# Gate and up products of a decoder layer taken by pairs of column chunks, three of eight k-tile pairs as 2 by 2 block products with seven multiplications

## The chip, the core and the metric

The kernel runs on one core of one Trainium2 chip. The metric is the device time of one execution in microseconds (us). The engines of the core are TensorE (PE in the profile, with its weight loads as PEld), VectorE (DVE), ScalarE (ACT), GpSimd (POOL) and SyncE (SP), whose queue issues most DMAs. SBUF is the memory that the engines read, PSUM the one that PE writes its products to, in eight banks of 128 partitions x 512 float32.

## The reference

One layer of a decoder for 256 tokens of width 2048, in float32. `w_gate` and `w_up` are 2048 x 5632, `w_down` is 5632 x 2048, and there are two feed-forwards:

```python
def swiglu(x, w_gate, w_up, w_down):
    return (jax.nn.silu(x @ w_gate) * (x @ w_up)) @ w_down

x = layer_norm(A * x + 0.5 * swiglu(x, ffn1 ...), ln1 ...)   # A = 2 ** 0.25
# token mixing: one input projection (2048 x 3416), 8 heads of latent attention,
# 8 heads of sparse attention with three gated branches, one output projection (2048 x 2048)
x = layer_norm(A * x + mix, ln2 ...)
x = layer_norm(A * x + 0.5 * swiglu(x, ffn2 ...), ln3 ...)
```

## The kernel before

**Three passes.** Each float32 operand is split into a high part of 12 bits and the rest. `split` (lines 74 to 76) does it with a cast on ACT (L75) and a subtraction on DVE (L76). A product of one k-tile, one token tile and one chunk of 512 columns is then `mm3` (lines 78 to 82): three matmuls, high by high (L80), high by low (L81), low by high (L82).

**Tiles.** The 256 tokens are two tiles of 128 (`t` = 0, 1). The 2048 inputs are 16 k-tiles of 128, loaded as eight pairs. The 5632 hidden columns are 11 chunks of 512. `load` (lines 120 to 138) brings a pair of k-tiles of one chunk, 512 KB, into a `raw` buffer (pool `rawp`, five) with a DMA on SP's queue, and splits it into `whi` and `wlo` (pools `hip` and `lop`, six buffers each of 128 x 1024).

**One product.** `gemm` (lines 143 to 183) takes one chunk of columns for both token tiles, each with a PSUM bank of the pool `acc` (four). Pair by pair it loads the weights and issues 2 k-tiles x 2 token tiles x 3 matmuls, then `finish` takes the banks. After each pair it calls `tick(2)`. The logical clock of ticks decides after which pieces the small side tasks (generators started by `spawn`) put their next instructions on PE; their banks come from the pool `msc` (four).

**Feed-forward.** `ffn` (lines 243 to 286) goes through the chunks in groups of 4, 4 and 3. For each chunk it does the gate product (`gate`: silu of the bank on ACT, L253), the up product (`up`: multiplied by the gate's result on DVE, L258), and `DFF` = 4 ticks later four transposes of that result for each token tile (L262), whose bank is split again into a `thi`/`tlo` pair. After a group, the down product accumulates the group's chunks, with `y` updated on DVE (L280, L282). `begin` and `after` load x, the constants and the residual in the first feed-forward; `late` calls `ln_res` (lines 342 to 350), which applies the gain and bias of the layer norm before to `y`, once for each of the first four chunks.

**Layer norm.** `ln` (lines 324 to 340) normalises `y` and transposes it by `norm_T` (lines 302 to 317) into the `x1` or `x2` pairs that the next products read. The first product after it takes eight pieces for token tile 0 before token tile 1 (`head`).

**What sets the order.** PE and SP run their instructions in the order of the program text. For DVE, ACT and POOL a planner orders the instructions when the kernel is built, by the order of the text and by its own estimate of when each is ready; the buffer of a pool that a tile gets is chosen in the same pass. Each engine then works its list in order. The order within a bank or a buffer is kept by semaphores.

Of the kernel before, what the change touches and what calls it, by code (L numbers as in the profile page):

```python
# [11 lines left out]
F32 = mybir.dt.float32  # L12
# [6 lines left out]
P = 128  # L19
D = 2048  # L20
S = 256
NT = S // P
# [14 lines left out]
NM = 12  # L37
DFF, DTR, DEV, DLN, DSM = 4, 7, 2, 4, 4
# [3 lines left out]
def layer(ctx: ExitStack, tc: tile.TileContext, a: dict, out: bass.AP):  # L42
# [4 lines left out]
    rawp = ctx.enter_context(tc.tile_pool(name="rawp", bufs=5))  # L47
# [11 lines left out]
    W = {n: (a[n], (k // P) // KT, w) for n, (k, w) in _CHUNKS.items()}  # L59

# [24 lines left out]
    lanes, now, flags = {}, [0], {}  # L85
# [34 lines left out]
    def load(w, c, pc, spare=False):  # L120
        """k-tiles pc of column chunk c of w, each as (hi, lo); `spare` takes them from the mixer's tiles"""
        ap, pairs, n = w
# [4 lines left out]
        nc.sync.dma_start(raw[:, :kn, :n], ap[r0:r0 + P].rearrange("p (k n) -> p k n", k=KT)[:, k0 % KT:k0 % KT + kn])  # L127
        if spare:
            out = []
            for j in range(kn):  # L130
                hi, lo = (am(F32R).rearrange("p a b -> p (a b)")[:, :n] for _ in range(2))
                split(hi, lo, raw[:, j, :n])
                out.append((hi, lo))
            return out
# [3 lines left out]
        return [(hi[:, j, :n], lo[:, j, :n]) for j in range(kn)]  # L138

    def new_acc():  # L140
        return acc.tile([P, NCH], F32, name="acc")

    def gemm(x, w, c, ks, finish, head=0, tail=0, spare=0, first=KT, each=None):
        """finish(t, ps): ps [128 tokens of tile t, n] = sum over k in ks of x[k, t].T @ w[k, column chunk c]

        The two token tiles alternate by piece of w, but for the first `head` and the last `tail` pieces,
        where tile 0 takes them all before tile 1.
        """
        n = w[2]
        ps = [new_acc()[:, :n] for _ in range(NT)]  # L150
# [33 lines left out]

    def new_T():
        return (tp.tile([P, 4, P], F32R, name="thi"), tp.tile([P, 4, P], F32R, name="tlo"))
# [10 lines left out]

    def load_x(k, n=2):
        """n k-tiles of x"""
        raw = rawp.tile([P, KT, NCH], F32, name="raw")  # L200
        nc.sync.dma_start(raw[:, :n, :S], a["xT"][k * P:(k + n) * P, :].rearrange("(k p) n -> p k n", p=P))
        for t in range(NT):
            if k % 4 == 0:
                xT[k // 4, t] = new_T()
            hi, lo = xT[k // 4, t]
            j = k % 4
            split(hi[:, j:j + n, :], lo[:, j:j + n, :], raw[:, :n, t * P:(t + 1) * P])

    def load_consts():
# [15 lines left out]
        # key k of the second half against query p: k <= p  # L225
# [17 lines left out]
    def ffn(wg, wu, wd, x, done, begin=None, after=None, late=()):  # L243
        groups = [[0, 1, 2, 3], [4, 5, 6, 7], [8, 9, 10]]
        late = list(late)
        for gi, grp in enumerate(groups):
            hT = {}
            for c in grp:
                sg = {}

                def gate(t, ps):
                    sg[t] = work.tile([P, NCH], F32, name="sg")
                    A.activation(sg[t], ps, AF.Silu)  # L253

                def up(t, ps):
                    def go(c=c, sg=sg):
                        h = wk([P, NCH])
                        V.tensor_tensor(h, ps, sg[t], op=OP.mult)  # L258
                        yield DFF
                        pt = msc.tile([P, 4, P], F32, name="msc")  # L260
                        for j in range(4):
                            PE.transpose(pt[:, j, :], h[:, j * P:(j + 1) * P], ident)  # L262
                        hT[c, t] = new_T()
                        split(hT[c, t][0], hT[c, t][1], pt)

                    spawn(go())
                    steps()

                gemm(x, wg, c, list(range(KD)), gate, head=0 if c or begin else HEAD, spare=SPARE,
                     first=1 if c == 0 and begin else KT, each=begin if c == 0 else None)  # L270
                gemm(x, wu, c, list(range(KD)), up, each=after if c == 0 else None)
                if late:
                    late.pop(0)()
# [28 lines left out]
    def norm_T(src, gcol, bcol, dst, k0):  # L302
        """dst (hi, lo) [128 k, j, 128 tok] <- transpose of src [128 tok, j*128] scaled by columns"""
        pt = msc.tile([P, 4, P], F32, name="msc")
# [12 lines left out]
        split(dst[0][:, :nj, :], dst[1][:, :nj, :], v[:, :nj, :])  # L317

# [5 lines left out]
    def ln(t, name, eps, x):  # L324
        """x[n, t] <- layer norm of y, transposed; y <- y normalised, without gain and bias"""
# [11 lines left out]
        for n in range(4):  # L337
            x[n, t] = new_T()
            norm_T(yc[n], cst[name + "_g"], cst[name + "_b"], x[n, t], 4 * n)
            yield 1  # L340

    def ln_res(name, n):
        """y, normalised so far, to the layer norm's result"""
# [34 lines left out]
    def done1(t, n):  # L378
# [5 lines left out]
    ffn(W["ffn1_w_gate"], W["ffn1_w_up"], W["ffn1_w_down"], lambda k, t: sl(xT[k // 4, t], k % 4), done1,  # L384
        begin=begin, after=load_y)

# [5 lines left out]
    def rope(dst, ps, cos, sin, h, d):  # L392
        """dst [128, h, d] <- rotated ps [128, h, d]"""
# [35 lines left out]
    def fin_b(t, ps):  # L429
        def go():  # L430
# [12 lines left out]
            pt = msc.tile([P, 4, P], F32, name="msc")  # L443
# [14 lines left out]
    def fin_c(t, ps):  # L458
        def go():
# [5 lines left out]
            pt = msc.tile([P, 4, P], F32, name="msc")  # L465
# [38 lines left out]
    def causal(ps, t, nh, scale, gate):  # L504
        """ps [128 q, nh*K] scores -> pT [128 keys, kb, nh, 128 q]"""
# [8 lines left out]
        pt = msc.tile([P, NCH], F32, name="msc")  # L514
# [15 lines left out]
    def mla_proj(g):  # L530
# [3 lines left out]
        def fin_q(hp):  # L534
            def fin(t, ps):
                def go():
# [6 lines left out]
                    pt = msc.tile([P, 4, P], F32, name="msc")  # L543
# [11 lines left out]
        def fin_kv(hp):  # L555
            def fin(t, ps):
                def go():
# [5 lines left out]
                    pt = msc.tile([P, 4, P], F32, name="msc")  # L563
# [17 lines left out]
    def mla_att(g, qnT, qrT, knT, vm):  # L581
        def unit(t, h0, nh):
# [3 lines left out]
            ps = msc.tile([P, NCH], F32, name="msc")  # L586
# [7 lines left out]
            po = msc.tile([P, 4, P], F32, name="msc")  # L594
# [10 lines left out]
    # native sparse attention  # L605
# [7 lines left out]
    def fin_kv2(n):  # L613
        def fin(t, ps):
            def go():
# [5 lines left out]
                pt = msc.tile([P, 4, P], F32, name="msc")  # L621
# [11 lines left out]
    def q_proj(g):  # L633
        def fin(t, ps):
            def go():
# [3 lines left out]
                pt = msc.tile([P, 4, P], F32, name="msc")  # L639
# [11 lines left out]
    # compressed keys and values  # L651
# [3 lines left out]
    def compress(src, n):  # L655
# [10 lines left out]
        pa = new_acc()  # L666
# [13 lines left out]
        pt = msc.tile([P, 4, P], F32, name="msc")  # L680
# [14 lines left out]
        po = msc.tile([P, 4, P], F32, name="msc")  # L695
# [12 lines left out]
    def nsa_att(g):  # L708
        pcTs = {}

        def cmp(t):
            yield from until(("q", g, t), ("kcmp",))
            qT = qTs[g, t]
            ps = msc.tile([P, 4, P], F32, name="msc")
# [7 lines left out]
            pt = msc.tile([P, 4, P], F32, name="msc")  # L722
# [6 lines left out]
        # selected blocks (all of them, as their number is at most SEL_TOPK) and window (wider than SEQ)  # L729
        def unit(t, h0, nh):  # L730
# [3 lines left out]
            for bi, n in ((1, "sel"), (2, "win")):  # L734
                yield from until(*[(n, b) for b in range(t + 1)])
                ps = msc.tile([P, NCH], F32, name="msc")
# [4 lines left out]
                if bi == 1:  # L741
                    yield from until(("pc", g, t), ("vcmp",))
                    po = msc.tile([P, 4, P], F32, name="msc")
# [29 lines left out]
    x2 = {}  # L773

    def out_last(ks, ns):
        """these columns for tile 0, then for tile 1"""
        held = {}
        for t in range(NT):
            for n in ns:
                ps = new_acc()  # L780
# [8 lines left out]
            spawn(ln(t, "ln2", LN_EPS, x2))  # L789
# [23 lines left out]
    def done3(t, n):  # L813
# [11 lines left out]
    ffn(W["ffn2_w_gate"], W["ffn2_w_up"], W["ffn2_w_down"], lambda k, t: sl(x2[k // 4, t], k % 4), done3,  # L825
        late=[lambda n=n: ln_res("ln2", n) for n in range(4)])
# [13 lines left out]
# weights: rows, columns of a chunk  # L840
_CHUNKS = {"w_in": (D, NCH), "w_in_b": (D, 344), "mla_w_uq": (QR, 384), "mla_w_ukv": (KVR, NCH), "w_out": (D, NCH)}
for _n in ("ffn1", "ffn2"):
    _CHUNKS.update({f"{_n}_w_gate": (D, NCH), f"{_n}_w_up": (D, NCH), f"{_n}_w_down": (FF, NCH)})

# [40 lines left out]
```

## Time and profile before

| | us |
|---|---|
| median of three runs | 1838.82 (1837.93 to 1839.55) |
| span of the profiled execution | 1836.4 |
| PE busy | 1819.7 |
| DVE busy | 1019.5 |
| ACT busy | 815.7 |
| mean DMA rate | 191 GB/s |

The span runs from the first to the last instruction of one profiled execution; no other time of that execution is listed, and the median of the runs is 2.4 us above the span. The busy time of an engine is the time in which at least one of its instructions runs. Matmuls are pipelined and overlap in the records, so the mean duration of one is longer than the time that it adds to a row of them.

### The profile page before, as it was taken

The page shows a single profiled execution, that of the slowest core. Times are in us where ns is not written, and L with a number is a line of the kernel's source. Part 1 is how long each engine was busy: PE and PEld are TensorE (multiplying, and loading weights), DVE is VectorE, ACT ScalarE, POOL GpSimd, SP SyncE. Part 2 cuts the span into 40 slices and gives each one's busy share as a digit, 9 for nine tenths or more (in the row PEclk, how much of TensorE's full clock was granted, in tenths as well). Part 3 has the DMA queues.
Part 4 walks back from the last instruction along what each step waited for, and adds up shares of the span by engine and source line. Part 5 has one row for each costly group of instructions (what it writes and reads, how often), then busy time and mean ns, then how long its engine had stood idle before and what let it go on. Part 6 is the DMA issues. An engine that isn't in the chain of part 4 may idle for free.

```text
span 1836.4 us, 21892 instructions
## 1 busy us (share of the span) xinstructions
PE 1819.7 (99%) x8394; PEld 1499.9 (82%) x8394; DVE 1019.5 (56%) x1253; ACT 815.7 (44%) x1071; POOL 17.7 (1%) x40
## 2 busy tenths in 40 slices
PE   8999999999999999999999999999999999999997
PEld 7888888888888888887788788888888888888886
DVE  5554554444554556766566687555455454545456
ACT  6444344444334444654555555444334444344431
POOL 0000000000000000000000000000000000000000
PEclk9999999999999999999999999999999999999999
DMA  9655565555555555566733347655665555555554
GB/s 341 226 194 174 193 204 194 186 184 183 195 195 185 193 186 182 170 186 217 267 104 127 126 161 231 201 187 185 194 195 194 185 194 186 194 193 189 191 192 138
DMA packets 102137, 349.98 MB, mean 191 GB/s; under 512 B 11136, under 2 KB 17296, under 8 KB 102032
## 3 DMA queue, kind: packets, MB, share of 16 engines
q1 hardware_dynamic: 100720, 344.37, 56.5%
q0 software_dynamic: 1312, 4.21, 1.0%
q8 instruction: 66, 1.08, 0.2%
q14 instruction: 39, 0.32, 0.1%
HBM read 346.44 MB, written 2.10 MB: 190 GB/s over the span
## 4 chain that ended last, share of the span: by engine, by line
PE 98%; DVE 1%; DMA 0%; ACT 0%; issue 0%; DVEq 0%; POOL 0%; ACTq 0%; POOLq 0%
PE acc L80 31%; PE acc L82 31%; PE acc L81 31%; PE msc L262 1%; PE msc L748 1%; PE msc L738 1%; PE msc L592 1%; PE acc L674 0%; PE msc L591 0%; PE msc L518 0%; PE msc L307 0%; PE msc L597 0%; DMA raw<-in_ffn_w_gate 0%; PE msc L745 0%; DVE wlo L76 0%
## 5 line engine op out<-in xcount | busy, mean ns | idle before, releaser
L76 DVE TENSOR_TENSOR wlo<-raw,whi 128x1024 fp32r<-128x1024 f32 (+3 forms) x604 | 733.3, 1215 | 721.5 <-ACT whi L75 720.3
L75 ACT CAST whi<-raw 128x1024 fp32r<-128x1024 f32 (+3 forms) x604 | 631.4, 1046 | 852.3 <-PE acc L82 805.7
L80 PE MATMUL acc<-whi,thi 128*128 128x512 f32 (+2 forms) x2414 | 945.2, 392 | 0.0
L81 PE MATMUL acc<-wlo,thi 128*128 128x512 f32 (+2 forms) x2414 | 936.3, 388 | 0.1
L82 PE MATMUL acc<-whi,tlo 128*128 128x512 f32 (+2 forms) x2414 | 936.4, 388 | 0.0
L80 PEld LDWEIGHTS acc<-whi,thi 128*128 128x128 f32 x2414 | 453.7, 188 | 95.7 <-issue 4.8
L82 PEld LDWEIGHTS acc<-whi,tlo 128*128 128x128 f32 x2414 | 453.4, 188 | 92.6
L81 PEld LDWEIGHTS acc<-wlo,thi 128*128 128x128 f32 x2414 | 453.8, 188 | 90.2 <-DVE wlo L76 0.8
L75 ACT CAST thi<-msc 128x512 fp32r<-128x512 f32 (+1 forms) x56 | 28.9, 556 | 37.4 <-PE msc L262 35.5
L80 PE MATMUL acc<-m,thi 128*128 128x512 f32 x98 | 39.2, 400 | 5.5 <-ACT m L75 4.7
L76 DVE TENSOR_TENSOR tlo<-msc,thi 128x512 fp32r<-128x512 f32 (+1 forms) x56 | 34.3, 645 | 17.6 <-ACT thi L75 17.6
L82 PE MATMUL acc<-m,tlo 128*128 128x512 f32 x98 | 38.9, 397 | 0.7 <-DVE tlo L76 0.7
L81 PE MATMUL acc<-m,thi 128*128 128x512 f32 x98 | 38.8, 396 | 0.0
L253 ACT ACTIVATE sg<-acc 128x512 f32<-128x512 f32 x44 | 26.3, 598 | 22.0 <-PE acc L82 21.9
L487 ACT ACTIVATE w<-w,mx 128x256 f32<-128x256 f32 (+1 forms) x48 | 21.4, 446 | 31.6 <-DVE mx L483 31.6
L76 DVE TENSOR_TENSOR m<-raw,m 128x512 fp32r<-128x512 f32 x49 | 31.6, 684 | 1.6 <-ACT m L75 1.6
L258 DVE TENSOR_TENSOR w<-acc,sg 128x512 f32<-128x512 f32 x44 | 28.3, 682 | 3.0 <-PE acc L82 3.0
L75 ACT CAST m<-raw 128x512 fp32r<-128x512 f32 x49 | 28.1, 617 | 2.7 <-DMA raw<-in_ffn_w_gate 2.7
L80 PEld LDWEIGHTS acc<-m,thi 128*128 128x128 f32 x98 | 18.7, 190 | 9.6 <-ACT m L75 4.7
L282 DVE TENSOR_TENSOR y<-acc,y 128x512 f32<-128x512 f32 x32 | 20.7, 682 | 9.9 <-PE acc L82 9.9
L82 PEld LDWEIGHTS acc<-m,tlo 128*128 128x128 f32 x98 | 18.7, 190 | 5.4 <-DVE tlo L76 1.6
L262 PEld LDWEIGHTS msc<-ident,w 128*128 128x128 f32 x176 | 20.5, 140 | 2.9
(144 smaller groups left out, 559.9 us busy)
## 6 DMA issues: line engine op xcount, KB each, us to landing
raw<-in_ffn_w_up SPq DMA_DIRECT2D x176, 512.0 KB, 3.3
raw<-in_ffn_w_down SPq DMA_DIRECT2D x176, 512.0 KB, 3.3
raw<-in_ffn_w_gate SPq DMA_DIRECT2D x175, 512.0 KB, 4.1
raw<-in_w_in SPq DMA_DIRECT2D x48, 512.0 KB, 4.4
raw<-in_w_out SPq DMA_DIRECT2D x32, 512.0 KB, 3.3
raw<-in_nsa_cmp_w_k SPq DMA_DIRECT2D x8, 512.0 KB, 4.1
raw<-in_nsa_cmp_w_v SPq DMA_DIRECT2D x8, 512.0 KB, 4.2
raw<-in_mla_w_uq SPq DMA_DIRECT2D x8, 384.0 KB, 3.9
```

The costliest lines, as they stand in the source:

```text
L75: A.copy(hi, src)
L76: V.tensor_tensor(lo, src, f(hi), op=OP.subtract)
L80: PE.matmul(ps, xh, wh, start=first, stop=False)
L81: PE.matmul(ps, xh, wl, start=False, stop=False)
L82: PE.matmul(ps, xl, wh, start=False, stop=last)
L253: A.activation(sg[t], ps, AF.Silu)
L258: V.tensor_tensor(h, ps, sg[t], op=OP.mult)
L262: PE.transpose(pt[:, j, :], h[:, j * P:(j + 1) * P], ident)
L282: V.tensor_tensor(y[t][:, cs], ps, y[t][:, cs], op=OP.add)
L487: A.activation(s[:, h, :], s[:, h, :], AF.Exp, bias=mx[:, h:h + 1], accum_out=sm[:, h:h + 1])
L592: PE.matmul(o, qrT[t][:, hh, :], krT[:, b, :], start=False, stop=True)
L738: PE.matmul(ps[:, h * K:(h + 1) * K], qT[:, h0 + h, :], kT[n][:, g, :K], start=True, stop=True)
```

## The change

**Algebra.** Chunks 0 to 9 of the gate and up weights are taken by pairs of chunks. For one pair of k-tiles (k, l), two token tiles and two chunks, the product is a 2 by 2 block product of eight `mm3`. In three of the eight pairs of k-tiles (`SEVEN` = 1, 3, 5) it is done with seven, in the way of Strassen and Winograd. With the weight blocks kn, lm, ln, km (k or l by chunk n or m) these are, by the bank that takes them:

- p1: x(k,0) kn; p5: s1 t1; p6: s2 t2; p7: s3 t3
- out(0,n): x(l,0) ln; out(0,m): s4 lm; out(1,n): x(l,1) t4; out(1,m): nothing
- t1 = kn + km, t3 = lm + km, t2 = t1 + lm, t4 = t2 + ln (three DVE instructions on raw weights, then split)
- s1 to s4: sums of the blocks of x, made once for each feed-forward in `sums`, split, and kept in six `m` tiles

After k-pair 5 DVE combines p1, p5, p6, p7 into four tiles (q = p6 + p1, u = p7 + q, v = p5 - q, z = p5 - u), and at the end of the product adds p1, v, u, z to the four output banks. The other five pairs take eight `mm3` into the four output banks.

**Where it is used.** `gemm2` does the gate products of the chunk pairs (2,3), (4,5), (6,7), (8,9) and the up products of those and of (0,1), in both feed-forwards. The gate products of chunks 0 and 1 stay with `gemm`, as do those of chunk 10 and all the others.

```diff
+NW = 11
+SEVEN = (1, 3, 5)
-    rawp = ctx.enter_context(tc.tile_pool(name="rawp", bufs=5))
+    rawp = ctx.enter_context(tc.tile_pool(name="rawp", bufs=6))
...
-    acc = ctx.enter_context(tc.tile_pool(name="acc", bufs=4, space=PSUM))
-    msc = ctx.enter_context(tc.tile_pool(name="msc", bufs=4, space=PSUM))
+    bank = ctx.enter_context(tc.tile_pool(name="bank", bufs=8, space=PSUM))
...
-        w = work.tile([P, NCH], F32, name="w", bufs=8)
+        w = work.tile([P, NCH], F32, name="w", bufs=NW)
...
+    def gemm2(x, xs, w, cp, finish, each=None):
+        ap = W2[w]
+        pairs = KD // KT
+        B = {}
+        todo = []
+        for i in range(pairs):
+            k, l = 2 * i, 2 * i + 1
+            if i in xs:
+                s1, s2, s3, s4 = (sl(xs[i], j) for j in range(4))
+                todo.append((i, [("p1", x(k, 0), "kn"), ((0, 1), s4, "lm"), ((0, 0), x(l, 0), "ln"), ("p5", s1, "t1"),
+                                 ("p7", s3, "t3"), ("p6", s2, "t2"), ((1, 0), x(l, 1), "t4")]))
+            else:
+                todo.append((i, [((t, j), x(kk, t), name) for name, kk, j in
+                                 (("kn", k, 0), ("lm", l, 1), ("ln", l, 0), ("km", k, 1)) for t in range(NT)]))
...
+        for i, ops in todo:
+            r0 = (cp * pairs + i) * P
+            full = [rawp.tile([P, KT, NCH], F32, name="raw") for _ in range(2)]
+            for j in range(2):
+                nc.sync.dma_start(full[j], ap[r0:r0 + P, 2 * j * NCH:2 * (j + 1) * NCH].rearrange("p (k n) -> p k n", k=KT))
+            a_, b_ = full
+            parts = [(a_, ("kn", "lm"), 2), (b_, ("ln", "km"), 1 if i in xs else 2)]
+            if i in xs:
+                t13 = rawp.tile([P, KT, NCH], F32, name="raw")
+                t24 = rawp.tile([P, KT, NCH], F32, name="raw")
+                V.tensor_tensor(t13, a_, b_[:, 1:2, :].broadcast_to([P, 2, NCH]), op=OP.add)
+                V.tensor_tensor(t24[:, 0], t13[:, 0], a_[:, 1], op=OP.add)
+                V.tensor_tensor(t24[:, 1], t24[:, 0], b_[:, 0], op=OP.add)
+                parts += [(t13, ("t1", "t3"), 2), (t24, ("t2", "t4"), 2)]
+            wt = {}
+            for src, names, n in parts:
+                hi = hip.tile([P, KT, NCH], F32R, name="whi")
+                lo = lop.tile([P, KT, NCH], F32R, name="wlo")
+                split(hi[:, :n], lo[:, :n], src[:, :n])
+                for j in range(n):
+                    wt[names[j]] = (hi[:, j], lo[:, j])
+            for o, (b, xp, name) in enumerate(ops):
+                if b not in B:
+                    B[b] = new_bank()
+                mm3(B[b], xp, *wt[name], first[b] == (i, o), last[b] == (i, o))
+            held[0] = i <= max(xs)
+            if i == max(xs):
+                p1, q, u, v, z = (wk([P, NCH]) for _ in range(5))
+                A.copy(p1, B["p1"])
+                V.tensor_tensor(q, B["p6"], p1, op=OP.add)
+                V.tensor_tensor(u, B["p7"], q, op=OP.add)
+                V.tensor_tensor(v, B["p5"], q, op=OP.subtract)
+                V.tensor_tensor(z, B["p5"], u, op=OP.subtract)
+                rest = {(0, 0): p1, (0, 1): v, (1, 0): u, (1, 1): z}
+            tick(2)
+            if each:
+                each(i)
+        for b, r in rest.items():
+            V.tensor_tensor(r, B[b], r, op=OP.add)
+            finish(*b, r)
...
+    def sums(v):
+        x11, x12, x21, x22 = v
+        s = wk([P, 4, P])
+        V.tensor_tensor(s[:, 0], x21, x22, op=OP.subtract)
+        V.tensor_tensor(s[:, 1], s[:, 0], x11, op=OP.subtract)
+        V.tensor_tensor(s[:, 2], x11, x21, op=OP.subtract)
+        V.tensor_tensor(s[:, 3], s[:, 1], x12, op=OP.add)
+        hl = am(F32R), am(F32R)
+        split(*hl, s)
+        return hl
...
+            def transposed(c, t, h):
+                def go():
+                    yield DFF
+                    while held[0]:
+                        yield 1
+                    pt = new_bank().rearrange("p (a b) -> p a b", a=4)
...
+            for c0 in grp[::2]:
+                cs = [c for c in grp if c // 2 == c0 // 2]
...
+                if c0 == 0 or len(cs) < 2:
+                    for c in cs:
+                        gemm(x, wg, c, list(range(KD)), gate(c), head=0 if c or begin else HEAD, spare=SPARE,
+                             first=1 if c == 0 and begin else KT, each=begin if c == 0 else None)
+                else:
+                    gemm2(x, xs, name + "_w_gate", c0 // 2, gate2)
+                if len(cs) < 2:
+                    gemm(x, wu, cs[0], list(range(KD)), up(cs[0]))
+                else:
+                    gemm2(x, xs, name + "_w_up", c0 // 2, up2, each=after if c0 == 0 else None)
+                for _ in cs:
+                    if late:
+                        late.pop(0)()
...
-    nc = bacc.Bacc("TRN2", target_bir_lowering=False, num_devices=1)
+    nc = bacc.Bacc("TRN2", target_bir_lowering=False, num_devices=1, dynamic_dma_scratch_size=4096)
```

**What else moves.** All PSUM tiles come from one pool of eight banks, `bank`, in place of `acc` and `msc`. While a product's four extra banks are in use (`held`, through k-pair 5) the transposes of finished hidden tiles wait. In `gate2` and `up2` the silu and the multiply read the sums from `w` tiles, where before they read the banks; the `sg` tiles are gone and there are 11 `w` tiles for 8. `sums` is called in `load_x` (first feed-forward) and, after token tile 1's `norm_T`, in the second layer norm. The weights of chunks 0 to 9 lie in memory by pairs of chunks, [kn, lm, ln, km] for each k-pair, so that each DMA of `gemm2` reads 4 KB runs; the gate's chunks 0 and 1, which `gemm` reads, come as two 2 KB runs a partition. The scratch for POOL's DMA descriptors is set to 4096.

More of the change, by code (lines that the diff above doesn't have):

```diff
@@ L126, in load @@
         raw = rawp.tile([P, KT, NCH], F32, name="raw")
-        nc.sync.dma_start(raw[:, :kn, :n], ap[r0:r0 + P].rearrange("p (k n) -> p k n", k=KT)[:, k0 % KT:k0 % KT + kn])
+        order = list(range(kn))
+        if len(w) > 3 and c < w[3][1]:
+            r0 = (c // 2 * pairs + k0 // KT) * P
+            src = w[3][0][r0:r0 + P].rearrange("p (i j n) -> p i j n", i=2, j=2)[:, :, c % 2, :]
+            if c % 2:
+                order = order[::-1]
+            if kn < KT:
+                at = k0 % KT if c % 2 == 0 else 1 - k0 % KT
+                src = src[:, at:at + 1]
+            nc.sync.dma_start(raw[:, :kn, :n], src)
+        else:
+            if len(w) > 3:
+                r0 = ((c - w[3][1]) * pairs + k0 // KT) * P
+            nc.sync.dma_start(raw[:, :kn, :n], ap[r0:r0 + P].rearrange("p (k n) -> p k n", k=KT)[:, k0 % KT:k0 % KT + kn])
         if spare:
@@ L133, in load @@
                 out.append((hi, lo))
-            return out
+            return [out[j] for j in order]
         hi = hip.tile([P, KT, NCH], F32R, name="whi")
@@ L137, in load, with new_bank @@
         split(hi[:, :kn, :n], lo[:, :kn, :n], raw[:, :kn, :n])
-        return [(hi[:, j, :n], lo[:, j, :n]) for j in range(kn)]
-    def new_acc():
-        return acc.tile([P, NCH], F32, name="acc")
+        return [(hi[:, j, :n], lo[:, j, :n]) for j in order]
+    def new_bank():
+        return bank.tile([P, NCH], F32, name="bank")
     def gemm(x, w, c, ks, finish, head=0, tail=0, spare=0, first=KT, each=None):
         n = w[2]
-        ps = [new_acc()[:, :n] for _ in range(NT)]
+        ps = [new_bank()[:, :n] for _ in range(NT)]
         pcs, i = [], 0
@@ L207, in load_x @@
             split(hi[:, j:j + n, :], lo[:, j:j + n, :], raw[:, :n, t * P:(t + 1) * P])
+        if k // KT in SEVEN:
+            xs0[k // KT] = sums([raw[:, j, t * P:(t + 1) * P] for t in range(NT) for j in range(2)])
     def load_consts():
@@ L240, in load_consts, with ffn @@
         return c
-    def ffn(wg, wu, wd, x, done, begin=None, after=None, late=()):
+    def ffn(name, x, xs, done, begin=None, after=None, late=()):
+        wg, wu = (W[name + n] + ((W2[name + n], _PAIRED[name + n]),) for n in ("_w_gate", "_w_up"))
+        wd = W[name + "_w_down"]
         groups = [[0, 1, 2, 3], [4, 5, 6, 7], [8, 9, 10]]
@@ L247, in ffn @@
             hT = {}
-            for c in grp:
-                sg = {}
[L251 to L273, printed above, removed]
+            def transposed(c, t, h):
[4 more added lines that the diff above has]
+                    pt = new_bank().rearrange("p (a b) -> p a b", a=4)
+                    for j in range(4):
+                        PE.transpose(pt[:, j, :], h[:, j * P:(j + 1) * P], ident)
+                    hT[c, t] = new_T()
+                    split(hT[c, t][0], hT[c, t][1], pt)
+                spawn(go())
+                steps()
@@ L302, in norm_T @@
     def norm_T(src, gcol, bcol, dst, k0):
-        pt = msc.tile([P, 4, P], F32, name="msc")
+        pt = new_bank().rearrange("p (a b) -> p a b", a=4)
         nj = src.shape[1] // P
@@ L338, in ln @@
             x[n, t] = new_T()
-            norm_T(yc[n], cst[name + "_g"], cst[name + "_b"], x[n, t], 4 * n)
+            v = norm_T(yc[n], cst[name + "_g"], cst[name + "_b"], x[n, t], 4 * n)
+            for j in range(2):
+                if xs is not None and 2 * n + j in SEVEN:
+                    xs.setdefault(2 * n + j, []).extend(v[:, 2 * j + i, :] for i in range(2))
+                    if t:
+                        xs[2 * n + j] = sums(xs[2 * n + j])
             yield 1
@@ L464, in go @@
             yield DTR
-            pt = msc.tile([P, 4, P], F32, name="msc")
+            pt = new_bank().rearrange("p (a b) -> p a b", a=4)
             for j in range(4):
@@ L513, in causal @@
         yield DSM
-        pt = msc.tile([P, NCH], F32, name="msc")
+        pt = new_bank()
         pv = pt[:, :nh * K].rearrange("p (b h q) -> p b h q", b=t + 1, h=nh)
@@ L542, in go @@
                     yield DTR
-                    pt = msc.tile([P, 4, P], F32, name="msc")
+                    pt = new_bank().rearrange("p (a b) -> p a b", a=4)
                     for j in range(2):
@@ L620, in go @@
                 yield DTR
-                pt = msc.tile([P, 4, P], F32, name="msc")
+                pt = new_bank().rearrange("p (a b) -> p a b", a=4)
                 for j in range(2):
@@ L638, in go @@
                 yield DTR
-                pt = msc.tile([P, 4, P], F32, name="msc")
+                pt = new_bank().rearrange("p (a b) -> p a b", a=4)
                 for j in range(4):
@@ L679, in compress @@
         yield 4
-        pt = msc.tile([P, 4, P], F32, name="msc")
+        pt = new_bank().rearrange("p (a b) -> p a b", a=4)
         for m in range(2):
@@ L694, in compress @@
         w2 = cst["w2_" + n]
-        po = msc.tile([P, 4, P], F32, name="msc")
+        po = new_bank().rearrange("p (a b) -> p a b", a=4)
         if n == "k":
@@ L713, in cmp @@
             qT = qTs[g, t]
-            ps = msc.tile([P, 4, P], F32, name="msc")
+            ps = new_bank().rearrange("p (a b) -> p a b", a=4)
             for h in range(4):
@@ L721, in cmp @@
             yield DSM
-            pt = msc.tile([P, 4, P], F32, name="msc")
+            pt = new_bank().rearrange("p (a b) -> p a b", a=4)
             for h in range(4):
@@ L735, in unit @@
                 yield from until(*[(n, b) for b in range(t + 1)])
-                ps = msc.tile([P, NCH], F32, name="msc")
+                ps = new_bank()
                 for h in range(nh):
@@ L823, in done3 @@
             ln_out(t, 4 * LN_EPS, gb3)
-    ffn(W["ffn2_w_gate"], W["ffn2_w_up"], W["ffn2_w_down"], lambda k, t: sl(x2[k // 4, t], k % 4), done3,
-        late=[lambda n=n: ln_res("ln2", n) for n in range(4)])
+    ffn("ffn2", lambda k, t: sl(x2[k // 4, t], k % 4), xs2, done3, late=[lambda n=n: ln_res("ln2", n) for n in range(4)])
     drain()
@@ L843 @@
     _CHUNKS.update({f"{_n}_w_gate": (D, NCH), f"{_n}_w_up": (D, NCH), f"{_n}_w_down": (FF, NCH)})
+_PAIRED = {f"{_n}_w_{_s}": 10 for _n in ("ffn1", "ffn2") for _s in ("gate", "up")}
 def kernel(**inputs):
```

64 lines of the change are left out of this document (49 added, 15 removed).

## The prediction

> **What bounds the kernel now.** I read the page's engine shares and chain first, then the longest pieces of the chain of waits in order of time, then the groups by shape, and last some stretches and the order of instructions.
>
> ```profile
> span 1836.4 us, 21892 instructions
> PE 1819.7 (99%) x8394; PEld 1499.9 (82%) x8394; DVE 1019.5 (56%) x1253; ACT 815.7 (44%) x1071; POOL 17.7 (1%) x40
> PE 98%; DVE 1%; DMA 0%; ACT 0%; issue 0%; DVEq 0%; POOL 0%; ACTq 0%; POOLq 0%
> L76 DVE TENSOR_TENSOR wlo<-raw,whi 128x1024 fp32r<-128x1024 f32 (+3 forms) x604 | 733.3, 1215 | 721.5 <-ACT whi L75 720.3
> L75 ACT CAST whi<-raw 128x1024 fp32r<-128x1024 f32 (+3 forms) x604 | 631.4, 1046 | 852.3 <-PE acc L82 805.7
> ```
>
> PE has work in 99% of the span and 98% of the chain. The other two engines wait for it in a ring: a cast (L75) waits for a `whi` buffer that PE gives back, the subtraction (L76) waits for the cast. So matmuls taken out shorten the span one for one, as long as the ring keeps up. What one matmul costs is read from the chain (start, length, what):
>
> ```profile
> 99.05 0.87 PE msc L262 x8
> 143.46 0.87 PE msc L262 x8
> 187.88 0.87 PE msc L262 x8
> ```
>
> Between two such marks lies one chunk of 512 columns: by the code 2 products x 8 k-pairs x 2 k-tiles x 2 token tiles x 3 passes = 192 matmuls and 8 transposes. (143.46 - 99.05 - 0.87) / 192 = **0.2268 us per matmul**. The profile's 0.39 us of one is a duration of overlapping instructions and isn't used.
>
> [...]
>
> **What goes.** `gemm2` takes the chunk pairs (2,3), (4,5), (6,7), (8,9) of gate and those and (0,1) of up: 9 products in each feed-forward, 18 in all. In each, three of eight k-tile pairs lose one block product, 3 matmuls: 18 x 3 x 3 = 162. 162 x 0.2268 = **-36.7 us**. A product of two chunks has (5x8 + 3x7) x 3 = 183 matmuls, 41.5 us, and half a pair's 1.74 us of transposes: 42.4 instead of 44.4. A seven-piece takes PE 21 x 0.2268 = 4.76 us, an eight-piece 5.44.
>
> **What is added on DVE and ACT.** Groups by shape, then stretches of DVE's timeline (start, length):
>
> ```profile
> L76 DVE TENSOR_TENSOR wlo<-raw,whi 128x1024 fp32r<-128x1024 f32 x587 | 718.2, 1224 | 705.2 <-ACT whi L75 704.0
> L75 ACT CAST whi<-raw 128x1024 fp32r<-128x1024 f32 x587 | 617.9, 1053 | 826.6 <-PE acc L82 796.1 <-DMA raw<-in_w_in 11.2 <-DMA raw<-in_ffn_w_up 7.6
> L258 DVE TENSOR_TENSOR w<-acc,sg 128x512 f32<-128x512 f32 x44 | 28.3, 682 | 3.0 <-PE acc L82 3.0
> L253 ACT ACTIVATE sg<-acc 128x512 f32<-128x512 f32 x44 | 26.3, 598 | 22.0 <-PE acc L82 21.9
> L75 ACT CAST m<-raw 128x512 fp32r<-128x512 f32 x49 | 28.1, 617 | 2.7 <-DMA raw<-in_ffn_w_gate 2.7
> ```
> ```profile
> 1103.01 1.22 DVE L76 TENSOR_TENSOR wlo<-raw,whi 128x1024 fp32r<-128x1024 f32 x1
> 1104.14 0.69 DVE L76 TENSOR_TENSOR tlo<-w,thi 128x512 fp32r<-128x512 f32 x1
> ...
> 1188.41 1.29 DVE L349 TENSOR_TENSOR y<-y,w 128x512 f32<-128x512 f32 x2
> 1189.62 1.28 DVE L350 TENSOR_TENSOR y<-y,w 128x512 f32<-128x512 f32 x2
> 1190.82 1.28 DVE L76 TENSOR_TENSOR tlo<-msc,thi 128x512 fp32r<-128x512 f32 x2
> ```
>
> From start to start, back to back, 1024 elements cost DVE 1104.14 - 1103.01 = 1.13 us and 512 cost (1189.62 - 1188.41) / 2 = 0.605. An eight-piece needs two wide subtractions, 2.26. A seven-piece needs one wide and two narrow sums of weights (the wide one has a broadcast operand, which no row shows; I take the plain wide price), three wide subtractions and one narrow: 1.13 + 2x0.605 + 3x1.13 + 0.605 = **6.3 us, more than PE's 4.76**. A product: 3x6.3 + 5x2.26 = 30.3; 4 combinations after k-pair 5 and 4 sums at its end, 8x0.605 = 4.8; 2.4 for the four up multiplies (as before) or the four splits of transposed tiles. **37.6 us of DVE against 42.4 of PE: 89%**, where it was 20.5 of 44.4 (16x1.13 + 2.4). Operations that wait for the one before don't overlap: 2x3 + 4 of them at 0.08 more, 38.4. ACT gains 1.05 + 0.62 in a seven-piece and one copy of 0.6 in a product, 5.6 in all, and stays far below.
>
> **Does it lie beside PE?** I count through one product with the six `whi` buffers in turn (2 for an eight-piece, 4 for a seven-piece). The buffer for `t13` of k-pair 3 is free when `t13` of k-pair 1 is multiplied, 8.8 us into the product, and due at 17.7. In those 8.8 us DVE owes the two subtractions of t13 and t24, two for pair 4 and the sums for pair 5: 4x1.13 + 2.34 = 6.9. It fits, with 1.9 to spare. From the end of pair 5 to the next product's first seven-piece PE has 3x5.44 + 1.74 = 18.1 us; DVE owes the combinations 2.4, four splits 2.4, four subtractions for pairs 7 and 0 4.5, 2.9 for three buffers of the next pair 1, its sums 2.3 and one end sum 0.6: 15.1. It fits too, so the forecast is that PE stays the bound. How crowded a DVE may be before PE feels it, two stretches tell (us, PE busy, PEld, DVE, ACT):
>
> ```profile
> 1088.00:1112.00 24.00, 23.08 (x116) 18.61 (x116) 21.19 (x41) 19.20 (x34) 1.86 (x3) 1.00 0.50 153
> 1096.00:1120.00 24.00, 24.00 (x115) 19.89 (x116) 19.75 (x35) 17.85 (x30) 2.94 (x5) 1.00 0.57 158
> ```
>
> At 82% PE lost nothing; at 88% it lost 0.92 of 24 us, 3.8%, though to the chain of a layer norm there. So crowding costs between 0 and 3.8% of 18 x 41.5, 28 us. I take 0.25 us a product, **+4.5**, near the low end, because the count above leaves slack at every due time.
>
> Places with more than that:
> - Last up product of a group, then down (or chunk 10): `DFF` = 4 ticks, two pieces, 5.44 us, until PE transposes. DVE owes 8 x 0.605 and one subtraction, 6.0. Six sites, 0 to 1.1 each (one subtraction more), taken 0.5: **+3**.
> - Two late `ln_res` now come together after the up products (0,1) and (2,3) of the second feed-forward: 8 x 0.605 = 4.8 us of DVE on top of 4.8 of ends and multiplies and 7.5 for pairs 1 to 3, in 10.2 us; some 7 late, of which pair 3's slack takes 6.5 (8.8 less a cast and a subtraction, 2.3). 0 to 2 each, taken 1: **+2**.
> - The second layer norm gains three `sums` (4 narrow operations and a split each, about 5 us of DVE) inside the first stretch above, between `norm_T`s whose results tile 1 waits for: 0 to 3, taken **+1**. Before the first feed-forward DVE has room.
> - The start. Gate chunks 0 and 1 are read in runs of 2 KB instead of 4.
>
> ```profile
> 0.00:46.00 46.00, 41.19 (x167) 33.07 (x168) 27.06 (x38) 28.31 (x43) 2.41 (x14) 1.00 0.94 341
> raw<-in_ffn_w_gate SPq DMA_DIRECT2D x175, 512.0 KB, 4.1
> raw<-in_ffn_w_gate SPq DMA_DIRECT2D x2, 256.0 KB, 3.4
> raw<-in_ffn_w_up SPq DMA_DIRECT2D x176, 512.0 KB, 3.3
> ```
>
> The DMA engines are 94% busy there. The two 256 KB loads have 2 KB runs already and aren't slow, so 0 to 3, one landing time; taken **+1**. Elsewhere bytes are the same and the runs 4 KB.
> - Shared banks (8 in turn instead of 4 and 4), three more `w` tiles and a smaller ring for POOL's DMAs touch the mixer. PE lost 1836.4 - 1819.7 = 16.7 us in all, start and end included, so a gain is at most a few us, a loss likewise (-2 to +2): 0.
>
> Sum: -36.7 + 4.5 + 3 + 2 + 1 + 1 = **-25.2**; span 1836.4 - 25.2 = 1811.2. The times shown are a median of 1838.8, 2.4 above this span (the profiled execution lists no other time of its own): **1813.6 us**.
>
> **Rivals.**
> *DVE paces the product.* DVE takes its list in the order the planner wrote. If that puts the subtractions of t13 and t24 right behind their casts, DVE stands 2 x 1.05 in each seven-piece: 37.6 + 6.3 = 43.9 to 44.7 a product, against 44.4 before: -9 to +5 over 18, **1837**. For it: the 721 us that L76 waits for casts today. Against it: today it waits because it has nothing else; the new list always has sums and ends to slip in between. It decides from (42.4 - 37.6) / 3 = 1.6 us of standing in a seven-piece.
> [...]
>
> *The raw buffers run dry (the slower side).* t13 and t24 take buffers of `rawp`, so in six buffers one seven- and one eight-piece fit. Were a seven-piece's loads issued only when the seven-piece before is being multiplied, the chain landing 3.3, wide sum 1.22, two narrow 1.36, cast 1.05, subtraction 1.22 = 8.2 would lie in line with 4.76 of PE: 12.9 instead of 10.2 for two pieces, 2.7 x 54 = +147, less 36.7: **1949**. It makes the kernel slower from 0.68 us for each seven-piece. For it: transfers land only 3.3 to 4.1 us after issue. Against: a raw buffer is given back at the subtraction, long before PE multiplies. By the count, pair 3's loads go out when pair 1's first matrix is subtracted (its cast may start 8.2 us before the product, so 5.9 before it); the cast of pair 3's t13 may start 8.8 into the product, 14.7 later, and landing and sums need 5.9.
>
> *All of it lands:* no losses, 1838.8 - 36.7 = **1802**. It needs a planner's order without a miss; it is the low end of my own case.
>
> **Numbers.** Forecast (PE-bound, losses 0 to 28) 0.75, its own range 1802 to 1830; DVE pacing 0.13; raw buffers 0.10; 0.02 for a change that saves no matmuls, as counted wrongly by me (1839). About 0.2% (3.7 us) is what a measurement of this kernel can tell from no change. Faster: 0.75 + 0.04 of the second = 0.79; same: 0.07 of the second and the 0.02, 0.09; slower: 0.10 + 0.02 = 0.12. All unknown losses at their ends, 28 + 6.6 + 4 + 3 + 3 + 2 = 47, would give 1849; together they are unlikely, and 1800 to 1845 leaves out that, and the raw case where it is full.
>
> **What would show it.** PE matmuls down by 162, marks of transposes about 84.7 us apart for a chunk pair (83.0 + 1.74); DVE's busy time up by 54 x 4.1 + 18 x 4.8 = some 310 to 1330 us, ACT's by some 100. PE idle for DVE (L76) under 20 us in sum. I am wrong if the marks lie 87 or more apart, if PE waits for `whi`, `wlo` or a bank at every seven-piece, or if the start or the second layer norm loses more than 5 us.

## The result

The changed kernel takes **1808.9 us** (median of 1807.5 to 1812.8) where the kernel before takes 1839.2: a ratio of 0.9835, with a 95% interval of 0.9822 to 0.9849. The prediction was 1813.6, within 1800 to 1845. The span of the profiled execution went from 1836.4 to 1805.8, 30.6 us less.

The page of the changed kernel, its engine shares, its chain and the two groups that made the ring of casts and subtractions (now lines 79 and 80):

```profile
span 1805.8 us, 22197 instructions
PE 1784.5 (99%) x8232; PEld 1470.5 (81%) x8232; DVE 1325.9 (73%) x1681; ACT 908.5 (50%) x1187; POOL 17.5 (1%) x40
PE 95%; DVE 3%; ACT 1%; issue 0%; DMA 0%; SPq 0%; POOL 0%; DVEq 0%; ACTq 0%; POOLq 0%
L79 ACT CAST whi<-raw 128x1024 fp32r<-128x1024 f32 (+3 forms) x728 | 730.9, 1015 | 786.2 <-PE bank L86 651.7
L80 DVE TENSOR_TENSOR wlo<-raw,whi 128x1024 fp32r<-128x1024 f32 (+3 forms) x728 | 842.8, 1175 | 380.8 <-ACT whi L79 377.7
L239 DVE TENSOR_TENSOR raw<-raw 128x1024 f32<-128x1024 f32 x54 | 66.0, 1222 | 16.7 <-DMA raw<-in_ffn_w_up 12.5
```

PE has 8394 - 8232 = 162 records fewer, the number counted from the code, and is still busy for 99% of the span. DVE has 306 us more work and still waits for casts, but half as long (378 us for 720). The wide sum with its broadcast operand (L239) takes 1.22 us, as the plain subtraction does.

The chain of waits of the changed kernel (start, length, what) shows what a product costs:

```profile
130.14 1.75 PE bank L359 x16
184.26 1.75 PE bank L359 x16
386.63 1.75 PE bank L359 x16
440.76 1.75 PE bank L359 x16
...
1207.15 1.75 PE bank L359 x16
1261.28 1.75 PE bank L359 x16
```

Between the first two marks PE works off, in order, 16 transposes (1.75), the last eight-piece of a gate product (24 matmuls), a whole paired up product (183) and two pieces of the down product (24): 231 x 0.2268 + 1.75 = 54.14. The marks are 54.12 apart, and the other three such pairs, two of them in the second feed-forward, lie 54.13 apart. **PE loses nothing in these paired up products.** In the other paired products the trace has one idle time of PE over 0.1 us, 1.50 us at 1176, which comes below. How full DVE is meanwhile, a stretch of each kernel tells (PE, PEld, DVE, ACT, POOL busy, granted clock, DMA share, GB/s), first before, then changed:

```profile
132.00:182.00 50.00, 50.00 (x226) 41.51 (x225) 23.46 (x22) 20.09 (x21) 0.00 (x0) 1.00 0.55 180
```
```profile
132.00:182.00 50.00, 50.00 (x222) 41.43 (x221) 43.88 (x52) 28.13 (x32) 0.00 (x0) 1.00 0.68 229
```

DVE went from 47% to 88%, and PE had no idle time beside it.

The 162 matmuls were priced at 36.7 us and the span is 30.6 shorter. The 6.1 us that are missing lie at three places. The start: the fourteenth matmul, from which on both chains run on PE without a break, begins at 11.73 us, where it began at 11.02, 0.7 later. The second layer norm: PE's timeline of the changed kernel there, with the wait ahead of an instruction in brackets, then stretches of it (the granted clock is the third number from the end):

```profile
1098.78 0.39 PE L86 MATMUL bank<-whi,tlo 128*128 128x512 f32 x1
1100.79 0.50 PE L84 MATMUL bank<-whi,thi 128*128 128x512 f32 x1 [1.63 <-ACT thi L79]
1101.13 0.40 PE L85 MATMUL bank<-wlo,thi 128*128 128x512 f32 x1
1101.88 0.56 PE L86 MATMUL bank<-whi,tlo 128*128 128x512 f32 x1 [0.35 <-DVE tlo L80]
1102.23 0.63 PE L84 MATMUL bank<-whi,thi 128*128 128x512 f32 x1
1102.66 0.63 PE L85 MATMUL bank<-wlo,thi 128*128 128x512 f32 x1
```
```profile
1102.00:1105.50 3.50, 3.50 (x9) 2.76 (x10) 3.50 (x4) 2.62 (x3) 0.54 (x1) 0.52 0.91 286
1105.50:1109.00 3.50, 3.50 (x16) 2.87 (x16) 2.09 (x2) 1.54 (x2) 0.00 (x0) 0.99 0.91 265
```

PE stands 1.63 us for the last x of token tile 1, which ACT and DVE deliver late because the sums of x are in between, and 0.35 us more. After that the clock is granted at 0.52 for some 3 us: matmuls start every 0.43 us, not every 0.23. Pauses and slow matmuls cost 4.1 us together, 2.5 the pauses and 1.6 the slow matmuls. The third place is the first paired gate product of the second feed-forward. ACT's, DVE's and PE's timelines there:

```profile
1175.35 2.95 ACT L79 CAST whi<-raw 128x1024 fp32r<-128x1024 f32 x3 [7.67 <-DVE raw L241]
```
```profile
1164.30 1.29 DVE L486 TENSOR_TENSOR y<-y,w 128x512 f32<-128x512 f32 x2
1165.50 1.29 DVE L487 TENSOR_TENSOR y<-y,w 128x512 f32<-128x512 f32 x2
...
1174.55 0.69 DVE L241 TENSOR_TENSOR raw<-raw 128x512 f32<-128x512 f32 x1
1175.16 7.50 DVE L80 TENSOR_TENSOR wlo<-raw,whi 128x1024 fp32r<-128x1024 f32 x7
```
```profile
1176.43 0.50 PE L85 MATMUL bank<-wlo,thi 128*128 128x512 f32 x1 [1.50 <-DVE wlo L80]
```

The two `ln_res` (L486, L487) and the ends of the up product stand in DVE's list ahead of the narrow sums of pair 1 (L241 is the last of them). DVE works without a break from 1164 on, ACT waits 7.67 us for the sums and PE 1.50: 1.8 us with the slower start after it. 0.7 + 4.1 + 1.8 = 6.6; the mixer became 0.3 us shorter, which leaves 6.3 against the 6.1 that are missing; the terms are read to some tenths.

### The profile page after: what moved, and what is told of

Read it like the earlier page. It is cut to its first block, busy times and chain, and to the rows that moved or that the text cites. A ratio compares the mean times of both kernels' runs of the same rounds, so it can differ in the third digit from the quotient of the medians.

```text
span 1805.8 us, 22197 instructions
## 1 busy us (share of the span) xinstructions
PE 1784.5 (99%) x8232; PEld 1470.5 (81%) x8232; DVE 1325.9 (73%) x1681; ACT 908.5 (50%) x1187; POOL 17.5 (1%) x40
## 4 chain that ended last, share of the span: by engine, by line
PE 95%; DVE 3%; ACT 1%; issue 0%; DMA 0%; SPq 0%; POOL 0%; DVEq 0%; ACTq 0%; POOLq 0%
PE bank L84 30%; PE bank L86 30%; PE bank L85 30%; PE bank L359 1%; PE bank L884 1%; DVE wlo L80 1%; PE bank L874 1%; PE bank L728 1%; PE bank L810 1%; PE bank L727 0%; PE bank L654 0%; DMA raw<-in_ffn_w_gate 0%; PE bank L733 0%; DVE tlo L80 0%; PE bank L881 0%
## 5 line engine op out<-in xcount | busy, mean ns | idle before, releaser
L79 ACT CAST whi<-raw 128x1024 fp32r<-128x1024 f32 (+3 forms) x728 | 730.9, 1015 | 786.2 <-PE bank L86 651.7
L80 DVE TENSOR_TENSOR wlo<-raw,whi 128x1024 fp32r<-128x1024 f32 (+3 forms) x728 | 842.8, 1175 | 380.8 <-ACT whi L79 377.7
L84 PE MATMUL bank<-whi,thi 128*128 128x512 f32 (+1 forms) x2208 | 864.8, 392 | 1.6 <-ACT thi L79 1.6
L85 PE MATMUL bank<-wlo,thi 128*128 128x512 f32 (+1 forms) x2208 | 856.7, 388 | 2.3 <-DVE wlo L80 2.3
L86 PE MATMUL bank<-whi,tlo 128*128 128x512 f32 (+1 forms) x2208 | 856.7, 388 | 0.3 <-DVE tlo L80 0.3
L84 PEld LDWEIGHTS bank<-whi,thi 128*128 128x128 f32 x2208 | 415.2, 188 | 90.4 <-issue 5.4
L85 PEld LDWEIGHTS bank<-wlo,thi 128*128 128x128 f32 x2208 | 415.4, 188 | 84.8 <-DVE wlo L80 3.3
L86 PEld LDWEIGHTS bank<-whi,tlo 128*128 128x128 f32 x2208 | 415.0, 188 | 85.1 <-DVE tlo L80 0.8
L85 PE MATMUL bank<-wlo,m 128*128 128x512 f32 x216 | 84.0, 389 | 0.0
L86 PE MATMUL bank<-whi,m 128*128 128x512 f32 x216 | 84.0, 389 | 0.0
L84 PE MATMUL bank<-whi,m 128*128 128x512 f32 x216 | 84.0, 389 | 0.0
L239 DVE TENSOR_TENSOR raw<-raw 128x1024 f32<-128x1024 f32 x54 | 66.0, 1222 | 16.7 <-DMA raw<-in_ffn_w_up 12.5
L241 DVE TENSOR_TENSOR raw<-raw 128x512 f32<-128x512 f32 x54 | 37.0, 686 | 0.2
L80 DVE TENSOR_TENSOR tlo<-bank,thi 128x512 fp32r<-128x512 f32 (+1 forms) x56 | 33.4, 644 | 0.4 <-ACT thi L79 0.4
```

What stands on the lines that cost most here:

```text
L79: A.copy(hi, src)
L80: V.tensor_tensor(lo, src, f(hi), op=OP.subtract)
L84: PE.matmul(ps, xh, wh, start=first, stop=False)
L85: PE.matmul(ps, xh, wl, start=False, stop=False)
L86: PE.matmul(ps, xl, wh, start=False, stop=last)
L239: V.tensor_tensor(t13, a_, b_[:, 1:2, :].broadcast_to([P, 2, NCH]), op=OP.add)
```

## The experiments

The theory (A): PE is the bound in every paired product, the gain is the matmuls alone, and the losses are the three places. The rivals: DVE is crowded everywhere and the three places only show it (B); the regrouping gives or costs something by itself; the raw buffers are near to running dry. Each ratio is to the kernel before, measured beside the run.

**Late sums.** In `ln`:

```diff
-                    if t:
-                        xs[2 * n + j] = sums(xs[2 * n + j])
             yield 1
+        if xs is not None and t:
+            yield 10
+            for i in SEVEN:
+                xs[i] = sums(xs[i])
+                yield 2
```

> The three sums of the second layer norm are made 10 ticks after its last transposed tile, and not between the tiles. Theory A (PE stays the bound in the products; the changed kernel's losses lie at three places: start 0.7, second layer norm 4.1 with the slow clock that follows, ln_res 1.8): the pause of 1.6 us at token tile 1's last x and the half-speed matmuls behind it go, about 4 us less than the changed kernel, 1805. Theory B (DVE is crowded everywhere, the pause is only where it shows): the work is only put off and stalls another place by about as much, 1809.

Measured: 1803.7 us, ratio 0.9808 (0.9795 to 0.9821), 5.2 less than the changed kernel. The stretch in which the pause was, first in the changed kernel, then here, where PE has work in all of it:

```profile
1092.00:1110.00 18.00, 16.02 (x63) 12.47 (x62) 14.19 (x24) 13.53 (x20) 1.12 (x2) 0.91 0.49 149
```

```profile
1092.00:1110.00 18.00, 18.00 (x81) 14.91 (x80) 14.20 (x26) 13.83 (x19) 0.96 (x2) 1.00 0.61 199
```

The span fell by 3.3, with a start 0.9 later in this kernel; from the end of the first feed-forward on it is 4.2 shorter, the 4.1 read from the trace. The work put off stalls no other place, so B, by which the loss would only move, falls here.

**Early ln_res.** The late calls move into the gate product of chunk 1:

```diff
-                             first=1 if c == 0 and begin else KT, each=begin if c == 0 else None)
+                             first=1 if c == 0 and begin else KT, each=begin if c == 0 else
+                             (lambda i: late.pop(0)() if late and i % 2 else None))
```

> The four ln_res of the second feed-forward are put into the gate product of chunk 1 (after every second piece), where DVE is half idle, and not two by two after paired up products. Theory A: the pause of 1.5 us in the first paired gate product of the second feed-forward goes, 1.8 us less, 1807; nothing else moves. Theory B: the hand-over from a paired up product to a paired gate product stalls by itself, at most 0.5 us less.

Measured: 1805.7, ratio 0.9816 (0.9802 to 0.9829). By the marks of the transposes the second feed-forward up to its first mark is 1.8 shorter, as read; the spans of the two profiled executions differ by 1.6 and the medians by 3.3. The changed kernel's four runs spread over 5.3 us and its profiled one was among the two fastest, so the rest is no more than that spread; no place of it is known. In the stretch where PE had waited, the changed kernel and then this one:

```profile
1150.00:1190.00 40.00, 38.49 (x170) 31.50 (x170) 36.72 (x45) 18.03 (x20) 1.08 (x2) 1.00 0.58 198
```
```profile
1150.00:1190.00 40.00, 40.00 (x178) 33.13 (x177) 36.69 (x42) 20.51 (x22) 0.00 (x0) 1.00 0.63 208
```

DVE is busy as long in both; what it does ahead of the sums has changed, and PE's pause is gone. B falls at this place too.

**Both.**

> Both edits. Theory A: the two add up, 6 us less than the changed kernel, 1803, which is 36 below the kernel before: nearly the whole price of 162 matmuls (36.7). Theory B: 0 to 2 us less.

Measured: **1801.9**, ratio 0.9797 (0.9783 to 0.9810), 7.0 less than the changed kernel; the span is 1800.8, 5.0 less. That is 37.4 below the kernel before measured beside it, the whole price of the 162 matmuls (36.7) within the interval. The distances of the marks haven't moved, 54.13:

```profile
130.65 1.75 PE bank L359 x16
184.78 1.75 PE bank L359 x16
```

This version beats both kernels.

**No sevens.** `SEVEN = ()`, the combinations after k-pair 5 are left out, nothing is held back, and in `gemm2`:

```diff
-        for b, r in rest.items():
-            V.tensor_tensor(r, B[b], r, op=OP.add)
+        for b in ((0, 0), (0, 1), (1, 0), (1, 1)):
+            r = wk([P, NCH])
+            V.tensor_copy(r, B[b])
             finish(*b, r)
```

> Chunks by pairs, shared banks, memory layout and pools as in the changed kernel, but all eight k-pairs with eight block products, no sums of weights or of x, and the four banks of a product copied to w tiles by DVE. Theory A: everything gained is the matmuls: 1839 (within 2 of the kernel before). A rival, that the regrouping by pairs or the shared banks give part of the gain: 1835 or less; that they cost something: over 1842.

Measured: 1838.7, ratio 0.9996 (0.9987 to 1.0005). Pairs of chunks, the new layout, the shared banks and the larger pools together are worth nothing by themselves; the gain is the multiplications.

**How much room has DVE?** The next two repeat the wide sum once and twice:

```diff
                 V.tensor_tensor(t13, a_, b_[:, 1:2, :].broadcast_to([P, 2, NCH]), op=OP.add)
+                V.tensor_tensor(t13, a_, b_[:, 1:2, :].broadcast_to([P, 2, NCH]), op=OP.add)
```

> The changed kernel with its wide sum (t13) done twice in each seven-piece, the same result written again: 1.13 us more of DVE in each, 41.0 us of DVE in a product against 42.4 of PE. By the prediction's bound (DVE decides from 1.6 us in a seven-piece): no more than 3 us slower than the changed kernel, 1809 to 1812, the most of it at the ln_res place. If DVE already paces the products: up to 54 x 1.13 = 61 us slower, and 20 or more at any rate.

> The wide sum done three times: 2.26 us more of DVE in each seven-piece, 44.4 us of DVE in a product against 42.4 of PE. By the prediction's bound DVE now paces the products: (44.4 - 42.4) x 18 = 36 us slower than the changed kernel, 1845, with PE waiting for wlo in every product. If DVE's room is larger than counted: under 10 us slower.

Measured: 1841.1, ratio 1.0012 (1.0002 to 1.0021), and 1868.6, ratio 1.0152 (1.0135 to 1.0169): 32 and 60 us slower than the changed kernel. **One more sum of 1.13 us in each seven-piece eats the whole gain.** The bound of 3 us failed. Behind the start PE's two longest waits are at the `ln_res` places, 3.6 and 5.1 us. Where it waits in a product, the run with one more sum shows (PE, then ACT, at k-pair 5 of an up product):

```profile
169.74 0.39 PE L86 MATMUL bank<-whi,tlo 128*128 128x512 f32 x1
170.39 0.50 PE L84 MATMUL bank<-whi,m 128*128 128x512 f32 x1 [0.26 <-ACT whi L79]
171.65 0.49 PE L85 MATMUL bank<-wlo,m 128*128 128x512 f32 x1 [0.76 <-DVE wlo L80]
```
```profile
163.78 0.62 ACT L79 CAST whi<-raw 128x512 fp32r<-128x512 f32 x1 [1.00 <-DMA raw<-in_ffn_w_up]
168.80 0.59 ACT L258 COPY w<-bank 128x512 f32<-128x512 f32 x1 [4.40 <-PE bank L86]
169.29 5.78 ACT L79 CAST whi<-raw 128x1024 fp32r<-128x1024 f32 x6
```

ACT stands 4.40 us in front of the copy of p1 (L258). p1 is finished only after PE's first block product of pair 5, and the casts of pair 5's t13 and t24 stand behind the copy in ACT's list, though DVE's sums for t13 had ended at 167.35. The planner, by its own estimate of the times, put the copy first. The row of these waits (us in total, times, the longest) in this run, then in the changed kernel:

```profile
ACT w L258 <- PE bank L86: 47.1, 13, 7.2
```
```profile
ACT w L257 <- PE bank L86: 0.4, 1, 0.4
```

So a new theory (O): a part of the loss is the order of the lists, not DVE's work.

**p6 copied first.** The copy is made to depend on a product that can only be finished after t13 and t24 have been cast:

```diff
-                A.copy(p1, B["p1"])
-                V.tensor_tensor(q, B["p6"], p1, op=OP.add)
+                A.copy(p1, B["p6"])
+                V.tensor_tensor(q, B["p1"], p1, op=OP.add)
+                A.copy(p1, B["p1"])
```

> The wide sum twice, as in the run with one more sum (1841), and p6 copied by ACT first (q = p1 + that copy) with p1's copy after it into the same tile: p6 is finished only after t13 and t24 have been multiplied, so the planner can't list the copy ahead of their casts. Theory O (list order): in the run with one more sum ACT stood 47 us at p1's copy, waiting for PE, with the due casts of t13 and t24 behind it; eleven pauses of 0.4 + 1.0 us at that place go, 17 us less: 1824, or less. Theory D (DVE is simply full from one more sum on): DVE has the same work, so 1838 to 1844.

> The wide sum three times and p6 copied first. Theory O: the share of the order goes, some 20 us, but DVE owes 44.4 in a product against 42.4 of PE, so the rest stays: 1845 to 1850. Theory D: 1865 or more. If it falls to 1830 or less, DVE's own work isn't what bounds it.

> Late sums, early ln_res and p6 copied first. With three sums ACT stood only 0.4 us at the copy, so theory O expects no change against late sums with early ln_res: 1801 to 1803. If one more copy of ACT in each product or the later release of the banks costs: 1804 or more.

Measured: with one more sum 1828.2, ratio 0.9940 (0.9924 to 0.9957), 12.9 less than without the reorder. With two more 1864.0, ratio 1.0134 (1.0119 to 1.0149), only 4.6 less. In the best version, where ACT's wait at the copy was short, 1803.4, ratio 0.9806 (0.9792 to 0.9821), 1.5 more. ACT's list at the same place, with one more sum:

```profile
165.93 1.05 ACT L79 CAST whi<-raw 128x1024 fp32r<-128x1024 f32 x1 [2.84 <-DVE raw L240]
167.38 2.01 ACT L79 CAST whi<-raw 128x1024 fp32r<-128x1024 f32 x2 [0.40 <-DVE raw L242]
170.69 0.59 ACT L258 COPY w<-bank 128x512 f32<-128x512 f32 x1 [1.31 <-PE bank L86]
```

The casts now come first and PE's pause at pair 5 is gone. What is left of the run with one more sum, 20.8 us of span, lies by the marks as follows: 5.9 in the first feed-forward, 3.4 up to the first mark of the second, 9.0 between that and the next mark, 2.5 behind it. Some 8 of the 9.0 are the second `ln_res` place, which in the changed kernel cost nothing:

```profile
1271.61 0.79 PE L85 MATMUL bank<-wlo,thi 128*128 128x512 f32 x1 [5.31 <-DVE wlo L80]
```

The 3.4 are 5.0 at the first `ln_res` place less 1.6, because here the pauses of the second layer norm (1.61 and 0.34 us) were not followed by slow matmuls. So of the 32 us about 13 were the order; by these marks about 12 are the two stretches with `ln_res` and some 8 the rest, on average about 0.5 us for a product (0.9 for an up product between marks). No run with one more sum moves the `ln_res`, so this division is read from the trace and not tested. D, that DVE is simply full, fits two more sums: the same stretch as above, with p6 first,

```profile
132.00:182.00 50.00, 47.46 (x215) 38.49 (x214) 48.29 (x53) 29.66 (x37) 0.00 (x0) 1.00 0.56 193
```

has DVE busy for 97% and PE idle for 2.5 of 50 us.

**Four sevens** (k-pairs 1, 3, 5, 6, with both edits of the best version), then with p6 first:

> Four seven-pieces (k-pairs 1, 3, 5, 6) instead of three, with the late sums and the early ln_res. 54 more matmuls go, 12.2 us. DVE then owes 4x6.3 + 4x2.26 + 7.2 = 41.5 in a product against PE's 40.8 + 0.9 = 41.7. Theory A: PE still bounds or nearly, 1803 - 12 = 1791 to 1800. If DVE paces a product once it is about as full as PE: it gives back 0.5 to 1 us in each of 18, 1800 to 1810.

> Four seven-pieces (1862) with p6 copied first. ACT stood 25 us at the copy there, and pairs of pauses of 0.4 + 1.0 us recur at pairs 5 and 6. Theory O: 15 to 25 us less, 1838 to 1847; what is left is pairs 5 and 6 standing side by side, where eight of the six buffers' turns fall together. Theory D: 1858 or more.

Measured: 1862.5, ratio 1.0123 (1.0108 to 1.0138), and 1840.4, ratio 1.0010 (1.0000 to 1.0019). 54 matmuls less made the kernel 61 us slower than the version with three. Copying p6 first takes off 22 of them; the rest stays. In that trace PE waits 1.9 to 2.3 us for a split (`wlo` or `m`, L80) at eight of the ten places behind a paired up product, within the first two pieces of the product that follows; why DVE is late there wasn't tested. The expectation had counted DVE and PE as equally full, 41.5 and 41.7 us, and taken that for a loss of 18 us at most.

**Five raw buffers** (`bufs=6` to `bufs=5`):

> The changed kernel with five raw buffers instead of six. If the raw buffers are near to running dry (the slower rival's mechanism): each seven-piece waits for its loads, 0.5 to 2.7 us, 27 us or more slower. By my count of the turns (loads go out about 9 us earlier than needed): one buffer less costs under 5 us in all.

Measured: 1835.6, ratio 0.9979 (0.9968 to 0.9991), 26.7 slower than the changed kernel. It isn't the loss that I had priced: in the first feed-forward a paired up product between two marks loses 0.5 us or nothing. The largest parts lie in the second feed-forward: 8.3 us between its first two marks, and 5.8 between the transposes of chunks 8 and 9 and those of chunk 10 (2.8 in the first). PE's longest wait is at the second `ln_res` place, between the first of these marks:

```profile
1274.91 0.79 PE L85 MATMUL bank<-wlo,thi 128*128 128x512 f32 x1 [4.48 <-DVE wlo L80]
```

Which step of the five buffers' turns is late there stays open.

## Why the prediction was right, and where it wasn't

- **The price of what goes** was right: 162 matmuls at 0.2268 are 36.7. Without sevens nothing is gained, and with two of the three losses removed 37.4 are, with an interval of about 35 to 40.
- **PE stays the bound:** right. DVE's share was forecast at 89% and measured at 88%; its busy time at 1330 and measured at 1326; ACT's at some 100 more and measured at 93 more.
- **The marks** don't lie 84.7 apart, as was said they would. The forecast took a chunk pair's gate and up products to lie between two marks; but the transposes of the first pair are held back until the next gate product is past k-pair 5, so only 231 matmuls lie between, and 54.1 us. As a sign it has to be read with these: 54.14 expected without a loss.
- **Crowding, +4.5:** measured 0. The two stretches from the layer norm gave a bound that had nothing to do with crowding, as the text suspected.
- **Group ends, +3:** measured 0. The operations fit into the two pieces; each of the four pairs of marks spans one of the six places and shows no loss, and at the other two PE has no idle time over 0.1 us.
- **ln_res, +2:** 1.8, though at one of the two places.
- **Start, +1:** 0.7. **Shared banks, 0:** -0.3.
- **Second layer norm, +1, at most 3:** 4.1. This is the term that was mis-sized. The place and the mechanism were right (sums ahead of `norm_T`s that tile 1 waits for), but the wait cost 2.5 where 1 was taken, and another 1.6 came afterwards as half-speed matmuls (one every 0.43 us, not every 0.23), which the price didn't have. This second part doesn't follow from the pauses alone: nearly the same two stand in the traces with one more sum, with and without p6 first, and with five raw buffers, with no slow matmuls behind them and 2.5 us lost.
- The sum of the losses was 11.5 for 6.1, so the span came out 5.4 under its forecast of 1811.2, and the median 4.7 under 1813.6. It came that near partly by luck: 7.5 were taken for crowding and group ends, which cost nothing, and 3.1 too little for the second layer norm.
- **The rival "DVE paces the product"** was much nearer than its chance of 0.13 said. Its point of decision, 1.6 us of standing in a seven-piece, was worked out from busy sums; in fact 1.13 us more cost the whole gain. What failed is the step from sums of work to slack: it left out that more DVE work makes the planner write another list, in which ACT stands in front of a product while due casts are behind it, and that places with extra work (`ln_res`) use the same slack a second time. With the list mended, one more sum cost about 0.5 us a product on average, so the count by turns was nearly right for the products alone. Two more cost more than it said: an up product between marks lost 3.5 where 44.4 - 42.4 = 2.0 was counted.
- This rival takes it that an engine works its list in order. ACT did so in the trace with one more sum: it stood 47.1 us in all, 13 times, in front of one kind of copy, and the copy at 168.80 had the cast of t13 behind it, whose sums had been ready since 167.35.
- **The rival "raw buffers"**: with six no loss in the products between marks is seen; with one less 26.7 us, where under 5 was expected. The count of turns looked at the seven-pieces and not at the hand-overs, where the largest losses appeared.

## What to carry to other kernels

Where one engine is busy for 99%, price a cut in its work from the distance between marks in its chain; that number held here, while stalls guessed for crowding didn't appear. Before trusting the slack on the second engine, look at what each list has behind an instruction that waits for the bound engine, and make such an instruction depend on something late enough. Put one-time work (sums, residuals) where the second engine is idle: moving two such pieces gave the last 5 us of span, and with one more sum the same work at a crowded hand-over went with a pause of 5 us.

## What the hardware showed that I hadn't expected

- A pause of PE of 1.63 us with another of 0.35 right behind it was followed by some 3 us at a granted clock of 0.52, with a matmul every 0.43 us, and cost 4.1 us. Nearly the same two pauses, 1.61 to 1.64 and 0.34 to 0.35 us, were followed by a granted clock of 1.00 in the traces with one more sum, with and without p6 first, and with five raw buffers, and cost 2.5. The pause of 1.50 us at 1176 wasn't followed by slow matmuls either: they start every 0.23 to 0.24 us. What decides between the two no run here shows.
- DVE at 88% busy cost PE nothing in 50 us of the changed kernel; with two more sums and p6 first, at 97%, PE was idle for 2.5 of the same 50 us.
